# The product with w_b_out by plain and block pairs, two low parts by DMA, and a turned order of matmuls in some products

## The chip, the core and the metric

One Trainium2 chip, one of its cores. The metric is the time of one execution on the device, in microseconds. The weights are in HBM, and a kernel is given them as they are. The host lays the activations with features on rows (1024 x 576: 512 frames of a new stream and 64 of a running one, 576 columns) and turns the outputs back.

## The reference

One layer of a streaming encoder: a half-step feed-forward, a mixer with two convolution branches, a second half-step feed-forward and a norm. All of it is float32.

```python
def encoder_layer(x, ...):
    x = x + 0.5 * swiglu_ffn(rms_norm(x, ffn1_norm), ffn1_w_gate_up, ffn1_w_down)   # 1024 -> 2 * 2816 -> 1024
    h = rms_norm(x, mix_norm)
    p = h @ w_in                                                                    # 1024 -> 7 * 1024
    a_b, a_c, a_v, b_u, gate_a, gate_b = jnp.split(p, cuts, axis=-1)
    a_conv, new_a = causal_depthwise_conv(a_c * a_v, hist_a, conv_a_w)              # 3 taps
    y_a = (a_b * a_conv) @ w_a_out
    glu = b_u[..., :D_B] * jax.nn.sigmoid(b_u[..., D_B:])
    b_conv, new_b = causal_depthwise_conv(glu, hist_b, conv_b_w)                    # 31 taps
    b_act = jax.nn.silu(layer_norm(b_conv + conv_b_bias, conv_b_ln_g, conv_b_ln_b))
    y_b = b_act @ w_b_out                                                           # 1024 -> 1024
    merged = jax.nn.sigmoid(gate_a) * y_a + jax.nn.sigmoid(gate_b) * y_b
    x = x + merged @ w_out
    x = x + 0.5 * swiglu_ffn(rms_norm(x, ffn2_norm), ffn2_w_gate_up, ffn2_w_down)
    return x, new_a, new_b
```

## The kernel before

**Layout.** Features are on partitions, in 8 tiles `X[0]` to `X[7]` of 128 x 576; the 576 columns are worked in two halves of H = 288. Every matmul takes 128 x 128 of a weight as the stationary operand and one half of an activation tile as the moving one, and it writes one half of a tile of PSUM. Operands are split into a high part (rounded to the format that TensorE multiplies in one pass) and a low part (the rest), and a product is hi*hi + hi*lo + lo*hi. So one chunk (128 rows of the sum) of one output tile is six matmuls, in the order of `SIX` (line 57): weight-high by x-high and x-low of half 0, the same of half 1, then weight-low by x-high of half 0 and of half 1. That is four matmuls with one weight and two with another. `mm` (line 396) issues them, `product` (line 444) runs all chunks of one output tile (8 chunks, 48 matmuls where the sum is over 1024), and `both` (line 470) runs two output tiles chunk by chunk.

**Block products.** For the gate and up projections of the feed-forwards the kernel uses seven products in place of eight (Winograd's form of Strassen's scheme): the two by two blocks are the two output tiles (or gate and up), the two halves of the sum and the two halves of the columns. `plan_block` (line 333) makes seven units of weights for such a pair: three plain ones and four sums `s1` to `s4` that DVE adds, each with a high and a low part. `Forms` (line 602) makes the matching combinations of the activations (`combine`: four DVE operations on halves and two ScalarE copies for the high parts; `split`: two DVE subtractions for the low parts), and `block` (line 417) runs one of the seven: 4 chunks of three matmuls, all into one bank of PSUM. A pair by blocks is 7 x 12 = 84 matmuls; two tiles the plain way are 96.

**Weights.** `Stream` (line 195) holds all weights in the order of their use. SyncE loads raw tiles (six buffers); `begin` makes the high part on ScalarE and, where the unit is "dma", lets ScalarE write its negative into the low tile and GpSimd issue a DMA that adds the raw weight on top; where it is "dve", `end` subtracts on DVE. Units are made `ahead` units before their use. Prepared weights live in tiles `u` and `g` (8 each) or `act` (44, shared with activations).

**Order of the mixer.** After feed-forward 1: products `("p", 4, j)` and `("p", 3, j)`, then 1, 2, 0; then `("p", 5, j)` and `("ya", j)` in turn (the branch A product, `ya_of` writes the gated result to `M[j]`), `("p", 6, j)` (gate of branch B), `("yb", j)` with w_b_out, and `("o", j)` with w_out, which adds to `X[j]` and scales for feed-forward 2. `swish` finishes branch B on DVE and ScalarE while `("p", 6, j)` runs; its operations wait in the list `work` and are put between products by `fill` and `gb_of`. Four times, `Sum.total` (line 552) sums squares or values over partitions: four matmuls with the weight `ones_r` put between two products (in feed-forward 1 it is six shorter ones, the `room` form).

The engines run in program order; which of them waits is decided by buffers and data alone.

Of the kernel before, what the change touches and what calls it, by code (L numbers as in the profile page):

```python
# [1 line left out]

# [11 lines left out]
P = 128  # L14
# [92 lines left out]
def tile_encoder_step(  # L107
# [19 lines left out]
    tmp = ctx.enter_context(tc.tile_pool(name="tmp", bufs=6))  # L127
    rpool = ctx.enter_context(tc.tile_pool(name="rpool", bufs=1))
    mmps = ctx.enter_context(tc.tile_pool(name="mmps", bufs=4, space=bass.MemoryType.PSUM))

# [64 lines left out]
    class Stream:  # L195
# [9 lines left out]

        def raw(self, w, row0, k, col0):
            ap = w[0, row0 : row0 + k * P, col0 : col0 + P].rearrange("(k p) n -> p k n", p=P)
            self.raws.append((ap, k))
            self.last.append({})
            return len(self.raws) - 1  # L210
# [102 lines left out]
    def plan_tile(name, w, row0, ks, col0, other, home_of=None, low="dma"):  # L313
        plan[name] = []
        for k in ks:
            r = ws.raw(w, row0, k, col0)
            plan[name].append(ws.unit(r, k, home_of or home(other), low))
            row0 += k * P
# [14 lines left out]
    def plan_block(name, raws, homes, low="dma"):  # L333
# [40 lines left out]

    def plan_mixer(name, w, col):
        plan_tile(name, w, 0, (KU, KU), col, "act")

# [6 lines left out]
    for j in range(KT):  # L384
        plan_mixer(("p", 5, j), w_in, 5 * D + j * P)
        plan_mixer(("ya", j), w_a_out, j * P)
    for j in range(KT):
        plan_mixer(("p", 6, j), w_in, 6 * D + j * P)
    for j in range(KT):
        plan_mixer(("yb", j), w_b_out, j * P)  # L390
    for j in IN_TURN:
        plan_mixer(("o", j), w_out, j * P)
    plan_ffn("f2", ffn2_gu, ffn2_dn)
# [23 lines left out]
    def block(w, xs):  # L417
# [6 lines left out]
        return q  # L424


    work = []
# [16 lines left out]
    def product(name, xs, then=None, order=None, got=None, soon=None):  # L444


        if name in early:
            return early.pop(name)[:, :, :H]
        ps = psum2()
        if order or got:  # L450
            got = got or chunks(name)
            for n, k in enumerate(order or range(len(xs))):
                mm(ps, *got[k], xs[k], n == 0, n == len(xs) - 1)
        else:
            k = 0
            for n in plan[name]:
                w = ws.get(n)
                for kk in range(ws.units[n][1]):
                    mm(ps, w, kk, xs[k], k == 0, k == len(xs) - 1)
                    k += 1  # L460
                    if soon and k == 1:
                        soon()
# [39 lines left out]
    class Sum:  # L502
# [49 lines left out]
        def total(self, spans=HALVES, room=None):  # L552

            if room:
# [47 lines left out]
    class Forms:  # L602

        def __init__(self, r_g):
            self.r_g, self.b, self.t, self.parts = r_g, {}, {}, {}
# [439 lines left out]
    def b_of(j):  # L1047
# [9 lines left out]
        return then  # L1057

    for j in range(KT):
# [11 lines left out]
    def swish(i, RL, sig={}):  # L1071
# [13 lines left out]
        if 0 <= j < KT:  # L1085
            BA[j] = (BA[j], low(sig[j], BA[j]))

    def ga_of(j):
# [5 lines left out]
    def ya_of(j):  # L1094
        def then(ps):
            m = atile() if j < 4 else wtile(n=T)
            dve.tensor_tensor(halves(m), ps, halves(gates.pop(j)), op=ALU.mult)
            M.append(m)
        return then
# [35 lines left out]
    while stage[0] < 4:  # L1135
        while work:
            work.pop(0)()
        advance()
    work.extend((lambda i=i: swish(i, RL)) for i in range(KT + 2))

# [11 lines left out]
    while work:  # L1152
        work.pop(0)()
    take()

    MS = []
    for j in range(KT):
        ps = product(("yb", j), BA)
        dve.tensor_tensor(halves(SGB[j]), ps, halves(SGB[j]), op=ALU.mult)
        dve.tensor_tensor(M[j], M[j], SGB[j], op=ALU.add)  # L1160
        MS.append(split(M[j]))
# [151 lines left out]
```

## Time and profile before

| | us |
|---|---|
| median of 3 runs | 1294.79 |
| lowest and highest | 1294.35, 1294.93 |
| the profiled execution's own time | 1294.93 |
| its span, first to last instruction | 1293.2 |
| TensorE busy | 1283.2 (99%) |
| DVE, ScalarE, GpSimd busy | 893.0, 763.5, 370.2 |

The span is what the trace covers; 1.7 us of the time lie around it. A matmul's shown length is modelled and overlaps the next one's, so the pace of TensorE is read from the starts: the time from the start of one group of matmuls to the start of the next, over their number.

### The profile page before, as it was taken

What the parts mean: (1) busy time and instruction counts of PE and PEld (TensorE: products, weight loads), DVE (VectorE), ACT (ScalarE), POOL (GpSimd) and SP (SyncE); (2) the same over time, 40 slices, a digit from 0 to 9 for tenths busy, and PEclk for the clock granted to TensorE, in tenths of its full rate; (3) what the DMA queues carried; (4) which work ended last, traced back from release to release, by engine and by line L of the source; (5) the groups of instructions that cost most, each with busy time, mean ns of one, the idle gap of its engine ahead of it and who ended that gap; (6) DMA issues with size and microseconds to landing.
All of it is one profiled execution on the core that took longest, in us unless ns stands there. A gap on an engine that the chain in (4) does not pass through costs nothing.

```text
span 1293.2 us, 25663 instructions
## 1 busy us (share of the span) xinstructions
PE 1283.2 (99%) x9752; PEld 1281.8 (99%) x9752; DVE 893.0 (69%) x1477; ACT 763.5 (59%) x1353; POOL 370.2 (29%) x470
## 2 busy tenths in 40 slices
PE   9999999999999999999999999999999999999997
PEld 9999999999999999999999999999999999999997
DVE  6858668748846998898885160346857858847956
ACT  7646656645776655555454674467665655654664
POOL 0032322322333444333321322222142241241230
PEclk9999999999999999999999999999999999999999
DMA  7286786886799898787885978776697696796683
GB/s 223 66 187 150 164 183 148 178 178 152 153 196 186 172 204 167 171 170 171 175 170 121 206 158 167 168 158 140 139 176 175 149 197 148 160 209 135 160 173 93
DMA packets 285948, 213.16 MB, mean 165 GB/s; under 512 B 15360, under 2 KB 248832, under 8 KB 285824
## 3 DMA queue, kind: packets, MB, share of 16 engines
q0 software_dynamic: 57600, 95.05, 44.7%
q1 hardware_dynamic: 226480, 115.63, 31.4%
q8 instruction: 77, 1.26, 0.4%
q10 hardware_dynamic: 1744, 0.83, 0.2%
q14 instruction: 47, 0.39, 0.1%
HBM read 113.81 MB, written 2.62 MB: 90 GB/s over the span
## 4 chain that ended last, share of the span: by engine, by line
PE 88%; issue 8%; DMA 2%; POOL 1%; DVE 1%; ACT 0%; POOLq 0%; DVEq 0%; SPq 0%; ACTq 0%
PE mm L83 88%; DMA u<-raw 1%; POOL g L83 1%; POOL u L83 1%; DMA raw<-in_ffn_w_gate_up_dram 0%; DMA raw<-in_ffn_w_down_dram 0%; DMA g<-raw 0%; DVE g L83 0%; DVE tmp L83 0%; POOLq L83 0%; DVE w L83 0%; DVEq L1303 0%; ACT g L83 0%; ACT u L83 0%; DVE r L83 0%
## 5 line engine op out<-in xcount | busy, mean ns | idle before, releaser
L83 PE MATMUL mm<-act,u 128*128 128x288 f32 x4686 | 660.3, 293 | 0.2 <-DMA u<-raw 0.2
L83 PEld LDWEIGHTS mm<-act,u 128*128 128x128 f32 x4686 | 630.7, 188 | 0.4 <-DMA u<-raw 0.4
L83 PE MATMUL mm<-act,g 128*128 128x288 f32 x2778 | 399.2, 294 | 0.0
L83 PEld LDWEIGHTS mm<-act,g 128*128 128x128 f32 x2778 | 377.9, 188 | 0.0
L83 PE MATMUL mm<-act,act 128*128 128x288 f32 (+2 forms) x2244 | 306.1, 293 | 0.0
L83 PEld LDWEIGHTS mm<-act,act 128*128 128x128 f32 x2244 | 297.4, 188 | 0.3 <-ACT act L83 0.3
L83 POOL DMA_DIRECT2D u<-raw x197 | 171.7, 871 | 411.3 <-ACT u L83 300.8
L83 ACT CAST u<-raw 128x512 fp32r<-128x512 f32 (+2 forms) x203 | 116.2, 572 | 155.8 <-PE mm L83 127.3
L83 POOL DMA_DIRECT2D g<-raw x117 | 101.9, 871 | 274.4 <-ACT g L83 220.0
L83 DVE SCALAR_TENSOR_TENSOR w<-g,prm,w 128x606 f32<-128x606 f32 x232 | 179.2, 842 | 1.4 <-ACT w L83 1.4
L83 DVE TENSOR_TENSOR tmp<-mm,tmp 128x288 f32<-128x288 f32 (+1 forms) x239 | 107.4, 458 | 68.1 <-PE mm L83 53.1
L83 POOL DMA_DIRECT2D act<-raw x86 | 73.9, 859 | 195.5 <-ACT act L83 186.3
L83 ACT ACTIVATE u<-u 128x512 fp32r<-128x512 f32 (+2 forms) x197 | 116.9, 593 | 6.3
L83 DVE SCALAR_TENSOR_TENSOR tmp<-mm,r 128x576 f32<-128x576 f32 x48 | 36.3, 756 | 79.1 <-PE mm L83 79.1
L83 ACT CAST g<-raw 128x512 fp32r<-128x512 f32 (+2 forms) x126 | 68.9, 547 | 37.2 <-DMA raw<-in_ffn_w_down_dram 16.7
L83 ACT CAST u<-w 128x512 fp32r<-128x512 f32 x79 | 48.9, 619 | 63.1 <-DVE w L83 55.4
L83 ACT CAST g<-w 128x512 fp32r<-128x512 f32 x77 | 47.7, 619 | 61.6 <-DVE w L83 55.5
L83 ACT CAST act<-tmp 128x576 fp32r<-128x576 f32 x84 | 56.7, 675 | 42.7 <-DVE tmp L83 41.1
L83 DVE TENSOR_TENSOR act<-tmp,act 128x576 fp32r<-128x576 f32 x84 | 62.1, 754 | 18.2 <-ACT act L83 16.5
L83 ACT ACTIVATE g<-g 128x512 fp32r<-128x512 f32 (+2 forms) x117 | 66.4, 568 | 3.7
L83 ACT CAST act<-raw 128x512 fp32r<-128x512 f32 (+3 forms) x94 | 55.4, 592 | 12.1 <-PE mm L83 6.5
L83 DVE TENSOR_TENSOR w<-raw,raw 128x512 f32<-128x512 f32 x78 | 53.4, 684 | 10.0 <-DMA raw<-in_ffn_w_gate_up_dram 10.0
(88 smaller groups left out, 802.0 us busy)
## 6 DMA issues: line engine op xcount, KB each, us to landing
raw<-in_ffn_w_gate_up_dram SPq DMA_DIRECT2D x171, 256.0 KB, 3.4
u<-raw POOLq DMA_DIRECT2D x140, 256.0 KB, 4.0
raw<-in_w_in_dram SPq DMA_DIRECT2D x112, 256.0 KB, 3.6
act<-raw POOLq DMA_DIRECT2D x80, 256.0 KB, 4.2
raw<-in_ffn_w_down_dram SPq DMA_DIRECT2D x96, 192.0 KB, 3.6
g<-raw POOLq DMA_DIRECT2D x60, 256.0 KB, 3.8
g<-raw POOLq DMA_DIRECT2D x43, 192.0 KB, 4.4
u<-raw POOLq DMA_DIRECT2D x41, 192.0 KB, 4.4
```

Source lines behind the costliest of these rows:

```text
L83: return self.tc.keep_in_program_order(fn(*args, **kwargs))
```

## The change

Three edits.

1. **The product with w_b_out.** The eight output tiles are made in four pairs: pairs 0 and 2 plain, pairs 1 and 3 by blocks. The combinations of branch B's activations are made by `Forms` from the outputs of `swish`: pairs 0 and 1 of them in the list `work`, 2 and 3 after the gate product. The low parts of the plain pairs' weights are made on DVE. To have room, `M[j]` is now `X[j]` itself: `X[j]` is written to HBM while products 1, 2, 0 run (`kept`), and read back (`back`) when `M[j]` has been split for the product with w_out. The prepared weights of the gate product go to `u` three times of four, and the units of w_out alternate between `u` and `g` rather than `u` and `act`.
2. **Two sums' low parts.** In the first two block pairs of feed-forward 2 (i = 1, 2) the low parts of `s3` and `s4` are made by DMA rather than by DVE.
3. **Turned chunks.** `turn` orders the matmuls of two neighbouring chunks anew: the first four of the first, all six of the second, the last two of the first. `both` does it at k = 1 with its two tiles (all eight places are the down products), `product` at chunks 1 and 2 where it is the first after a `Sum.total` without `room`, and in the first product with w_out. The up product of feed-forward 2, which follows a total too, is handed its weights (`got`) and takes the other branch: it clears the mark and is not turned.

```diff
-        ], [home("g") for _ in range(7)], "dve" if (f, i) == ("f1", PLAIN[f]) else "dma")
+        ], [home("g") for _ in range(7)], "dve" if (f, i) == ("f1", PLAIN[f]) else "dma",
+            "dma" if f == "f2" and i < PLAIN[f] + 2 else "dve")
...
-                (s3, "dve", ((s3, (a11, a21)),)),
+                (s3, low_s, ((s3, (a11, a21)),)),
                 (a12, low, ()),
-                (s4, "dve", ((s4, (s2, a12)),)),
+                (s4, low_s, ((s4, (s2, a12)),)),
...
+    for i in range(KU):
+        pair = 2 * i, 2 * i + 1
+        if i % 2 == 0:
+            for j in pair:
+                plan_mixer(("yb", j), w_b_out, j * P, homes_b, "dve")
+        else:
+            plan_block(("yb", "s", i), [
+                ws.raw(w_b_out, h * P, KU, j * P, 2) for j in pair[::-1] for h in range(2)
+            ], [next(homes_b) for _ in range(7)])
     for j in IN_TURN:
-        plan_mixer(("o", j), w_out, j * P)
+        plan_tile(("o", j), w_out, 0, (KU, KU), j * P, "g")
...
+    def turn(tiles, xs):
+        (p, w, k, x), (q, v, l, z) = ((*t, x) for t, x in zip(tiles, xs))
+        for ps, u, kk, b, six in (p, w, k, x, SIX[:4]), (q, v, l, z, SIX), (p, w, k, x, SIX[4:]):
+            mm(ps, u, kk, b, False, False, six=six)
+    turned = [False]
...
         ps = psum2()
+        at, turned[0] = 1 if turned[0] else None, False
...
+                    if k == at:
+                        turn([(ps, w, kk), (ps, w, kk + 1)], xs[k : k + 2])
+                    elif at is None or k != at + 1:
+                        mm(ps, w, kk, xs[k], k == 0, k == len(xs) - 1)
...
         for k in range(len(xs)):
+            if k == 1:
+                turn([(p, *w[k]) for p, w in zip(ps, ws_)], [xs[k]] * 2)
+                continue
...
             p = psum2()
+            turned[0] = True
             span = slice(spans[0][0], spans[-1][1])
...
     for j in range(KT):
         for b, of in ((1, c_of), (2, cv_of), (0, b_of)):
             product(("p", b, j), xg, of(j))
-    M, SGB, BA = [], [], []
+        nc.sync.dma_start(kept[j], X[j])
+    M, SGB, BA = X, [], []
+    forms = Forms()
...
+    for i in range(KT + 2):
+        work.append(lambda i=i: swish(i, RL))
+        if i in (3, 5):
+            work.append(lambda p=(i - 3) // 2: forms.combine(p))
+        if i in (4, 6):
+            work.append(lambda p=(i - 4) // 2: forms.split(p))
+    ws.ahead = 4
...
+    def merged(j, c):
+        dve.tensor_tensor(M[j], M[j], c, op=ALU.add)
+        if j not in (4, 5):
+            MS[j] = high(M[j])
+            if j != KT - 2:
+                lows(KT - 2, KT - 1) if j == KT - 1 else lows(j)
...
+        for n, xs in enumerate(bs):
+            q.append(block(ws.get(plan["yb", "s", i][n]), xs))
+            if n > 0:
+                steps[n - 1]()
+        dve.tensor_tensor(half(c2, 0), q[6], u3, op=ALU.add)
+        dve.tensor_tensor(c2, c2, SGB[j + 1], op=ALU.mult)
+        merged(j + 1, c2)
...
+    plain_pair(0)
+    block_pair(1)
+    plain_pair(2)
+    back(0, 1)
+    block_pair(3)
+    back(2, 3)
...
+    turned[0] = True
     for n, j in enumerate(IN_TURN):
         ps = product(("o", j), MS)
+        if n < 2:
+            back(4 + 2 * n, 5 + 2 * n)
```

## Rows read from the trace of the kernel before

**Rows 1.** The page: busy time of the engines, and the granted TensorE clock in 40 slices of the span.

```profile
PE 1283.2 (99%) x9752; PEld 1281.8 (99%) x9752; DVE 893.0 (69%) x1477; ACT 763.5 (59%) x1353; POOL 370.2 (29%) x470
PEclk9999999999999999999999999999999999999999
```

**Rows 2.** All waits of TensorE that the trace shows (us in total, times, longest).

```profile
PE mm L83 <- POOL eps L83: 1.0, 1, 1.0
PE mm L83 <- ACT tmp L83: 0.5, 1, 0.5
PE mm L83 <- DMA u<-raw: 0.2, 1, 0.2
```

**Rows 3.** Timeline of TensorE (start, modelled length, groups of like matmuls) at the end of feed-forward 1's down products, through the first product with w_in (two rows of 24), the first total (4 matmuls), and the next product.

```profile
386.10 2.54 PE L83 MATMUL mm<-act,g 128*128 128x288 f32 x18
...
395.57 3.32 PE L83 MATMUL mm<-act,act 128*128 128x288 f32 x24
398.74 3.33 PE L83 MATMUL mm<-act,u 128*128 128x288 f32 x24
401.90 0.69 PE L83 MATMUL mm<-tmp,ones_r 128*128 128x288 f32 x4
402.43 3.28 PE L83 MATMUL mm<-act,act 128*128 128x288 f32 x24
405.55 3.28 PE L83 MATMUL mm<-act,u 128*128 128x288 f32 x24
408.67 3.28 PE L83 MATMUL mm<-act,act 128*128 128x288 f32 x24
```

**Rows 4.** The same view around the two totals of the layer norm: a row before and after the first, then a row before and after the second.

```profile
686.35 3.29 PE L83 MATMUL mm<-act,u 128*128 128x288 f32 x24
689.47 0.69 PE L83 MATMUL mm<-tmp,ones_r 128*128 128x288 f32 x4
690.00 3.32 PE L83 MATMUL mm<-act,act 128*128 128x288 f32 x24
693.16 3.32 PE L83 MATMUL mm<-act,u 128*128 128x288 f32 x24
...
715.28 0.69 PE L83 MATMUL mm<-tmp,ones_r 128*128 128x288 f32 x4
715.81 3.28 PE L83 MATMUL mm<-act,act 128*128 128x288 f32 x24
718.93 1.33 PE L83 MATMUL mm<-act,u 128*128 128x288 f32 x9
```

**Rows 5.** The same view, the product with w_b_out: its first and last of 16 rows of 24 matmuls, and the first row of the product with w_out.

```profile
796.93 3.28 PE L83 MATMUL mm<-act,act 128*128 128x288 f32 x24
...
843.73 3.28 PE L83 MATMUL mm<-act,u 128*128 128x288 f32 x24
846.85 1.33 PE L83 MATMUL mm<-act,act 128*128 128x288 f32 x9
```

**Rows 6.** The same view, the start of feed-forward 2: the total, the plain up product (two rows of 24), the first block pair (its first row of seven and the first row of the next pair), and the start of the down products.

```profile
903.02 0.69 PE L83 MATMUL mm<-tmp,ones_r 128*128 128x288 f32 x4
903.55 3.32 PE L83 MATMUL mm<-act,g 128*128 128x288 f32 x24
...
909.87 1.74 PE L83 MATMUL mm<-act,g 128*128 128x288 f32 x12
...
920.99 1.74 PE L83 MATMUL mm<-act,u 128*128 128x288 f32 x12
...
954.35 4.90 PE L83 MATMUL mm<-act,g 128*128 128x288 f32 x36
...
962.25 2.54 PE L83 MATMUL mm<-act,g 128*128 128x288 f32 x18
```

**Rows 7.** The same view, two other places where the rhythm of six is broken: the `room` total in feed-forward 1, and the last total but one at the end.

```profile
24.89 0.81 PE L83 MATMUL mm<-tmp,ones_r 128*128 128x192 f32 x6
...
27.93 3.32 PE L83 MATMUL mm<-act,u 128*128 128x288 f32 x24
31.09 3.19 PE L83 MATMUL mm<-act,g 128*128 128x288 f32 x23
...
1274.25 0.47 PE L83 MATMUL mm<-tmp,ones_r 128*128 128x304 f32 x2
1274.56 8.68 PE L83 MATMUL mm<-act,act 128*128 128x272 f32 x69
1283.08 0.62 PE L83 MATMUL mm<-acc,ones 128*128 128x272 f32 x2
```

**Rows 8.** Busy time by stretch (length, then PE, PEld, DVE, ACT, POOL with counts, granted clock, DMA share, GB/s): the gate product with w_in, the product with w_b_out, the block pairs of feed-forward 2's first group.

```profile
747.00:797.00 50.00, 50.00 (x387) 50.00 (x386) 21.80 (x33) 33.18 (x53) 12.90 (x15) 1.00 0.82 168
797.00:847.00 50.00, 50.00 (x387) 50.00 (x386) 15.91 (x21) 23.74 (x40) 13.75 (x16) 1.00 0.73 157
904.00:953.00 49.00, 49.00 (x372) 49.00 (x372) 41.94 (x75) 33.93 (x62) 13.03 (x16) 1.00 0.66 138
```

**Rows 9.** DVE's groups in the block pairs of feed-forward 2 (operation, shapes, count, busy, mean ns): steps from PSUM, low parts of combinations, low parts and sums of weights.

```profile
L83 DVE TENSOR_TENSOR tmp<-mm,tmp 128x288 f32<-128x288 f32 (+1 forms) x23 | 10.4, 463 | 4.3 <-ACT tmp L83 3.3 <-PE mm L83 1.0
L83 DVE TENSOR_TENSOR act<-tmp,act 128x576 fp32r<-128x576 f32 x8 | 5.8, 753 | 0.5
L83 DVE TENSOR_TENSOR u<-w,u 128x512 fp32r<-128x512 f32 x8 | 5.5, 684 | 0.1
L83 DVE TENSOR_TENSOR w<-raw,raw 128x512 f32<-128x512 f32 x7 | 4.8, 682 | 0.0
```

**Rows 10.** DVE's timeline at the product with w_b_out: the gating of its first tile (in brackets DVE's idle time before it, and what ended that), then the last tile's gating, its add, and the low part for w_out.

```profile
803.37 0.76 DVE L83 TENSOR_TENSOR w<-mm,w 128x576 f32<-128x576 f32 x1 [31.27 <-PE mm L83]
...
847.05 0.76 DVE L83 TENSOR_TENSOR g<-mm,g 128x576 f32<-128x576 f32 x1 [3.19 <-PE mm L83]
847.84 0.76 DVE L83 TENSOR_TENSOR w<-w,g 128x576 f32<-128x576 f32 x1
849.35 0.76 DVE L83 TENSOR_TENSOR act<-w,act 128x576 fp32r<-128x576 f32 x1 [0.74 <-ACT act L83]
```

**Rows 11.** DMA issues on SyncE's queue (KB each, us from issue to landing).

```profile
raw<-in_w_b_out_dram SPq DMA_DIRECT2D x16, 256.0 KB, 3.1
x<-in_x_dram SPq DMA_DIRECT2D x8, 288.0 KB, 5.5
```

More of the change, by code (lines that the diff above doesn't have):

```diff
@@ L1 @@
+from collections.abc import Iterator
 from contextlib import ExitStack
+from itertools import cycle
 import concourse.bass as bass
@@ L204, in __init__, with raw @@
             self.sums, self.eager = {}, False
-        def raw(self, w, row0, k, col0):
-            ap = w[0, row0 : row0 + k * P, col0 : col0 + P].rearrange("(k p) n -> p k n", p=P)
-            self.raws.append((ap, k))
+        def raw(self, w, row0, k, col0, step=1):
+            rows = w[0, row0 : row0 + k * P] if step == 1 else w[0]
+            ap = rows[:, col0 : col0 + P].rearrange("(k a p) n -> a p k n", a=step, p=P)
+            self.raws.append((ap[row0 // P if step > 1 else 0], k))
             self.last.append({})
@@ L316, in plan_tile @@
             r = ws.raw(w, row0, k, col0)
-            plan[name].append(ws.unit(r, k, home_of or home(other), low))
+            to = next(home_of) if isinstance(home_of, Iterator) else home_of or home(other)
+            plan[name].append(ws.unit(r, k, to, low))
             row0 += k * P
@@ L373, in tile_encoder_step, with plan_mixer @@
     plan_ffn("f1", ffn1_gu, ffn1_dn)
-    def plan_mixer(name, w, col):
-        plan_tile(name, w, 0, (KU, KU), col, "act")
+    def plan_mixer(name, w, col, home_of=None, low="dma"):
+        plan_tile(name, w, 0, (KU, KU), col, "act", home_of, low)
     for j in range(KT):
@@ L386, in tile_encoder_step @@
         plan_mixer(("ya", j), w_a_out, j * P)
+    few = cycle(("u", "u", "u", "act"))
     for j in range(KT):
-        plan_mixer(("p", 6, j), w_in, 6 * D + j * P)
-    for j in range(KT):
-        plan_mixer(("yb", j), w_b_out, j * P)
+        plan_mixer(("p", 6, j), w_in, 6 * D + j * P, few)
+    homes_b = iter((
+        "u", "act", "u", "act", "u", "act", "u", "act", "u", "g", "act",
+        "u", "act", "u", "g", "u", "act", "u", "g", "u", "act", "g",
+    ))
+    for i in range(KU):
[7 more added lines that the diff above has]
+            ], [next(homes_b) for _ in range(7)])
     for j in IN_TURN:
-        plan_mixer(("o", j), w_out, j * P)
+        plan_tile(("o", j), w_out, 0, (KU, KU), j * P, "g")
     plan_ffn("f2", ffn2_gu, ffn2_dn)
@@ L1057, in b_of @@
         return then
+    kept = [
+        dram.tile([P, T], F32, tag=f"kept{j}", name=f"kept{j}") for j in range(KT)
+    ]
     for j in range(KT):
@@ L1153, in tile_encoder_step, with back @@
         work.pop(0)()
+    for p in range(KU // 2, KU):
+        forms.combine(p)
     take()
[L1156 to L1161, printed above, removed]
+    for p in range(KU // 2, KU):
+        forms.split(p)
+    MS = [None] * KT
+    def back(*js):
+        for j in js:
+            nc.sync.dma_start(X[j], kept[j])
@@ new lines, in tile_encoder_step, with lows, plain_pair @@
+    ws.ahead = AHEAD_UNITS
+    bs = forms.operands(BA[::2] + BA[1::2])
+    def lows(*js):
+        for j in js:
+            MS[j] = MS[j], low(M[j], MS[j])
+    def merged(j, c):
[4 more added lines that the diff above has]
+                lows(KT - 2, KT - 1) if j == KT - 1 else lows(j)
+    def plain_pair(i):
+        for j in (2 * i, 2 * i + 1):
+            ps = product(("yb", j), BA)
+            dve.tensor_tensor(halves(SGB[j]), ps, halves(SGB[j]), op=ALU.mult)
+            merged(j, SGB[j])
@@ new lines, in block_pair, with second, first @@
+    def block_pair(i):
+        j = 2 * i
+        c1, c2, qu, uu = (ttile() for _ in range(4))
+        q1, u2, u3, u4 = half(qu, 0), half(qu, 1), half(uu, 0), half(uu, 1)
+        q = []
+        def second():
+            dve.tensor_tensor(u3, q[3], u2, op=ALU.add)
+            dve.tensor_tensor(half(c2, 1), u3, q[2], op=ALU.subtract)
+            if i == KU - 1:
+                MS[4], MS[5] = split(M[4]), split(M[5])
+        def first():
+            dve.tensor_tensor(half(c1, 1), q[5], u4, op=ALU.add)
+            dve.tensor_tensor(c1, c1, SGB[j], op=ALU.mult)
+            merged(j, c1)
+        steps = (
+            lambda: sca.copy(q1, q[0]),
+            lambda: dve.tensor_tensor(u2, q[1], q1, op=ALU.subtract),
+            lambda: dve.tensor_tensor(u4, q[2], u2, op=ALU.subtract),
+            second,
+            lambda: dve.tensor_tensor(half(c1, 0), q[4], q1, op=ALU.add),
+            first,
+        )
+        for n, xs in enumerate(bs):
[5 more added lines that the diff above has]
+        merged(j + 1, c2)
+        spare.clear()
@@ L1163, in tile_encoder_step @@
+    plain_pair(0)
[4 more added lines that the diff above has]
+    back(2, 3)
+    ss = Sum()
+    xg = [None] * KT
+    forms = Forms(R_N2)
     ss = Sum()
```

12 lines of the change are left out of this document (5 added, 7 removed).

## The prediction

> **What bounds the kernel now.** I read the page first: TensorE is busy for 99% of the span at the full granted clock, the 2.4 GHz level, and no other engine is over 69% [rows 1]. Then TensorE's waits: all that it waited for is 1.7 us, most of it at the two ends [rows 2]. So the time is the number of matmuls times their pace, and only three things move it: fewer matmuls, another pace, or a new wait.
>
> The pace has to be read from starts in the timeline, and there the reader should see what the page hides. All these matmuls have 288 columns and one granted clock, but they run at different paces. Products by `SIX` have two, which I call the short beat (130.0 ns a matmul) and the long beat (131.67). In feed-forward 1's down products and the first product with w_in, 48 matmuls take 401.90 - 395.57 = 6.33 us, 131.9 ns each, the edge of the total included; the next product takes 408.67 - 402.43 = 6.24 us, 130.0 each [rows 3]. Down products: (395.57 - 386.10)/72 = 131.5. For the long beat I use the 3.16 us per 24 matmuls from 690.00 to 693.16 [rows 4], 131.67 ns. The change of pace falls on the total: four matmuls with one weight, put between two chunks. The total at 689.47 turns short into long, the one at 715.28 turns long into short [rows 4], and the one at 903.02 turns short into long: the up product behind it takes 909.87 - 903.55 = 6.32 us [rows 6]. So TensorE has two beats, 1.67 ns a matmul apart; a run of like chunks keeps its beat for hundreds of us, and four more matmuls of one weight toggle it. Blocks have a longer one still: 920.99 - 909.87 = 11.12 us for 84, 132.4 ns [rows 6]. They are seen only where the long beat came in, and the down products behind them have it too.
>
> **Edit 1, matmuls.** The product with w_b_out takes 846.85 - 796.93 = 49.92 us for 384 matmuls, 130.0 each, all in the short beat [rows 5]. Two pairs go from 2 x 96 = 192 to 2 x 84 = 168 matmuls. 192 x 130.0 = 24.96 us become 168 x 132.4 = 22.24 us: **-2.7 us**. Bounds of the new pace: 130.0, if blocks keep the short beat (-3.1), and 132.4. I take 132.4, since that is every block in the trace. The plain pair between the two block pairs then finds the long beat: 96 x 1.67 = **+0.2 us**. Pair 0 stays at 130.0.
>
> **Edit 1, what else it moves.** All of this must stay under TensorE. DVE is busy for 15.9 of 50 us in this product [rows 8]. Added: low parts of 8 units of the plain pairs, 8 x 0.68; in the block pairs 8 sums and 8 low parts of sums, 16 x 0.68; 14 steps on halves, 14 x 0.46 [rows 9]: 22.9 us, together 38.8 in about 47.4 us, 82%. The block pairs of feed-forward 2 run with DVE at 41.9 of 49 us, 86% [rows 8], and TensorE has no wait there [rows 2], so I cost it at nothing. The combinations: 4 x (4 x 0.46 + 2 x 0.75) = 13.4 us of DVE. DVE was idle for 31.27 us before 803.37, since 772 [rows 10], and has 21.8 of 50 us in the gate product [rows 8]; the combinations are needed from about 809, so they fit. If `swish` ended only with the gate product, the last two combinations (6.7 us) would still lie under plain pair 0 (12.5 us of matmuls). `kept` and `back` are 16 more transfers of 288 KB on SyncE's queue; the like took 5.5 us to land [rows 11]. The writes wait for nothing. The reads wait for the low parts of `M[j]`, and the weight loads stand behind them; `back(4, 5)` waits longest, until late in the last block pair, but the weights then in the buffers are six units ahead, over 9 us even at a block's 1.6 us each, and `X[4]` is needed only after two products of 6.2 us. Nothing, and if a load does come late, a wait of the size of one landing (3.1 us [rows 11]). In return ten of the sixteen low parts by DMA leave GpSimd's queue.
>
> **The tightest place** is the start of the product with w_out, which needs all of `M` split. Now the low part of the last tile ends 850.11 - 846.85 = 3.3 us after the last matmul [rows 10] and is needed at the eighth chunk, 42 x 0.130 = 5.5 us after it. With the last block pair there is one half step (0.46) more on this chain, one low part (0.76) more, because tiles 6 and 7 are split together, and the gating of tile 6 ahead of it ends about 0.5 us late: 3.3 + 0.46 + 0.76 - 0.74 (the wait for ScalarE [rows 10], which the other low part now fills) + 0.45 = 4.2 us. 1.3 us are left, so nothing; if ScalarE is held by a weight copy at that moment, two operations of 0.62 us, it is even.
>
> **Edit 2.** Four low parts, 4 x 0.68 = 2.7 us, leave DVE at the start of feed-forward 2, and ScalarE and GpSimd get four more each. DVE does not hold TensorE there [rows 2, 8], so nothing either way; the room on ScalarE (33.9 of 49 us) covers 4 x 0.63.
>
> **Edit 3, the turns.** No matmul more or less; all it can move is the beat. The trace holds no turn, so its worth is bounded from both sides by the two paces: at one end all `SIX` products in the long beat go over to the short one, at the other all in the short beat to the long one. What speaks for a change to the short beat: a turn puts, behind complete chunks, four matmuls with one weight and then a complete chunk, which is just what a total does [rows 3, 4]. What speaks against: the two matmuls left over follow, and two of one weight changed the pace as well at the end: 69 matmuls of 272 columns take (1283.08 - 1274.56)/69 = 123.5 ns, near their 113.3 of columns plus the 10 that the short beat has over 120 [rows 7]. And six matmuls of 192 columns did not toggle it: the products behind have the long beat (31.09 - 27.93 = 3.16 us per 24) [rows 7]. I take it that a turn ends in the short beat. It is nearer to the totals than to the other two in shape and columns.
>
> Then, at 1.67 ns: feed-forward 1's down products, 1056 matmuls less 24 at each of the four starts, 960 x 1.67 = **-1.6**. The first product with w_in, 48: **-0.1**. The first total then finds the short beat and leaves the long one, and the turn in the next product mends it after 18 matmuls: 0. The four products from 690.00 to 715.28, 192 matmuls less 20: **-0.3**; after the second total 18 in the long beat: 0. Product with w_out: turned behind the block pair, so 130.0 as now: 0. The up product of feed-forward 2 is not turned, so 131.67 as now: 0. Feed-forward 2's down products: first three groups 768 less 72, 696 x 1.67 = **-1.2**; the last group has its own halves of 304 and 272 columns and a last total that would now toggle the other way: its 108 first matmuls give 0.1, the end may take 0.1 back: **-0.1**.
>
> **Sum.** -2.7 + 0.2 - 1.6 - 0.1 - 0.3 - 1.2 - 0.1 = -5.8 us. The profiled execution took 1294.9, 0.1 above the median of 1294.8, so I predict **1289.0** beside that median.
>
> **Rivals.**
> - *Order does not matter.* Pace would hang on columns alone, or a turn undo itself with its last two matmuls. Then the block pairs leave the long beat for the product with w_out and the first of feed-forward 2, 432 x 1.67 = +0.7, and the next total gives the up product the short beat, -0.1: -2.7 + 0.2 + 0.7 - 0.1 = -1.9, **1292.9**. For it: the 192-column total and the left-over two. Against it: three toggles at one column count and one clock. The Trainium skill, TensorE: Matmul & The Clock Gate, section "Back-to-back issue gap", puts a warm matmul alone at columns/2.4 + 2.5 ns, whatever stands before it; by that, an estimate, 288 columns are 122.5 ns and a turn is worth nothing. The trace does not agree: 130.0, 131.67 and 132.4 ns.
> - *Blocks keep the short beat.* The 17 pairs behind turned down products in each feed-forward, and the two new ones, go to 130.0: 36 x 84 x 2.4 ns = 7.3 us more, **1281.7**. For it: the last 69 matmuls, three to a chunk as in a block, have the short beat [rows 7]. Against it: it asks that blocks, which were never seen in it, hold it through changes between halves.
> - *Down products gain, the projection loses.* The turn in the down products works, so the first total now leaves the long beat; the turn inside one `product` stands at another phase (one chunk before it, not two) and fails. 402.43 to 689.47 is 2208 matmuls, +3.7; the stretch to 715 gains 0.3; then 720 matmuls +1.2, and w_out +0.7. With the rest: **about 1294.6**.
> - *The other side: a turn spoils what a total has mended.* If the down products stay at 131.67, the first total still leaves 130.0, and a turn that toggles puts the whole projection at 131.67: +3.7, after the second normal total +1.2, w_out +0.7; -2.7 + 0.2 + 3.7 + 1.2 + 0.7 = +3.1, **1297.9**. It decides as soon as a turn behind the first total ends in the long beat, for that alone is more than the block pairs save.
>
> **How the numbers follow.** Chances: forecast 0.57, order without effect 0.15, blocks at 130.0 0.08, down gains and projection loses 0.10, spoiled 0.10. 0.2%, 2.6 us, is about what a measurement can tell from no change here. Faster by more: forecast and blocks at 130.0, 0.65. Within: 0.25. Slower: 0.10. The forecast's own range is 1287.5 to 1291.0: the bounds of the new blocks' pace below, a wait of a us or two at w_out above. 1286.0 to 1294.9 takes in the forecast and the two cases above it, 0.82; the two outer ones are left out.
>
> **What would show it.** In the timeline of TensorE: rows of 12 for two stretches of about 11.1 us in the product with w_b_out, which as a whole is near 47.4 us; 3.12 us per 24 matmuls in down products, at 402 to 715 and in w_out; 2.37 us per 18 in down products would mean that the turn did nothing. In the waits: nothing new on TensorE; a wait on `act` at the first product with w_out would show that the tightest place did not hold. Wrong altogether if a row of 24 behind the first total is 3.16 us.

## The result, and the profile after

The changed kernel takes 1297.0 us (median of 18 executions, 1293.9 to 1298.3) against 1294.8 before: 1.0016 times as long, interval 1.0009 to 1.0022. The forecast was 1289.0. The profiled execution of after took 1297.2 us with a span of 1295.2, 2.0 more than before's.

No engine's load explains it. From the page of after, the answer to [rows 1]:

```profile
PE 1283.5 (99%) x9728; PEld 1281.9 (99%) x9728; DVE 922.9 (71%) x1535; ACT 768.0 (59%) x1363; POOL 365.9 (28%) x464
PEclk9999999999999999999999999999999999999999
```

TensorE has 24 matmuls fewer and the same full clock, and is busy for 0.3 us longer: the pace got worse. Where, the starts in its timeline tell. The ledger is made of differences between starts, after less before ([rows 3 to 6] and the fences below; f1 and f2 are the two feed-forwards):

| stage | forecast | measured |
|---|---|---|
| to the first total (f1 down, first w_in product) | -1.7 | 400.22 - 401.90 = -1.68 |
| first total to first total of the layer norm | 0 | 291.28 - 287.57 = +3.71 |
| between that and the second one | -0.3 | 25.83 - 25.81 = +0.02 |
| second total to the product with w_b_out | 0 | 82.71 - 81.65 = +1.06 |
| product with w_b_out | -2.5 | 47.53 - 49.92 = -2.39 |
| w_out and the first product of f2, to the total of f2 | 0 | 56.94 - 56.17 = +0.77 |
| total of f2 to its down products | 0 | 53.48 - 51.33 = +2.15 |
| f2 down products to the end | -1.3 | 2.0 less the sum above = -1.6 |

Each row compares one profiled execution with one other, so small differences are within the spread: to the first total, the ten profiled kernels with the turned pairs take 399.68 to 401.09 us, the three without them 401.90 to 402.20.

Timeline of TensorE in after, around the first total and the two of the layer norm (start, modelled length, group; against [rows 3, 4]):

```profile
397.10 3.29 PE L85 MATMUL mm<-act,u 128*128 128x288 f32 x24
400.22 0.69 PE L85 MATMUL mm<-tmp,ones_r 128*128 128x288 f32 x4
400.75 3.34 PE L85 MATMUL mm<-act,act 128*128 128x288 f32 x24
403.94 3.33 PE L85 MATMUL mm<-act,u 128*128 128x288 f32 x24
407.10 3.33 PE L85 MATMUL mm<-act,act 128*128 128x288 f32 x24
...
691.50 0.69 PE L85 MATMUL mm<-tmp,ones_r 128*128 128x288 f32 x4
692.03 3.34 PE L85 MATMUL mm<-act,act 128*128 128x288 f32 x24
...
717.33 0.69 PE L85 MATMUL mm<-tmp,ones_r 128*128 128x288 f32 x4
```

The row ahead of the first total is 3.12 us (400.22 - 397.10): the turns in the down products brought the short beat. Behind it the row with the turn is 3.19 us and the next 407.10 - 403.94 = 3.16. Behind the other two totals the ledger says the same: nothing gained between the totals of the layer norm (+0.02), and 624 matmuls x 1.67 ns = 1.04 of the 1.06 us lost behind the second. The turn inside a product did not mend what the total did. The prediction had named a row of 3.16 us behind the first total as what would make it wrong altogether.

The product with w_b_out and the start of feed-forward 2 (same view; the last number in brackets is idle time and what ended it; against [rows 5, 6]):

```profile
800.04 3.33 PE L85 MATMUL mm<-act,u 128*128 128x288 f32 x24
...
812.68 1.74 PE L85 MATMUL mm<-act,u 128*128 128x288 f32 x12
...
823.80 3.33 PE L85 MATMUL mm<-act,u 128*128 128x288 f32 x24
...
845.97 4.94 PE L85 MATMUL mm<-act,g 128*128 128x288 f32 x36
...
904.51 0.69 PE L85 MATMUL mm<-tmp,ones_r 128*128 128x288 f32 x4
...
915.00 1.82 PE L85 MATMUL mm<-act,g 128*128 128x288 f32 x12 [0.30 <-DVE tmp L85]
...
924.79 1.58 PE L85 MATMUL mm<-act,u 128*128 128x288 f32 x10 [1.36 <-DMA u<-raw]
...
957.99 4.89 PE L85 MATMUL mm<-act,g 128*128 128x288 f32 x36
```

The block pair takes 823.80 - 812.68 = 11.12 us, as forecast. (The row of 36 at 845.97 is a block's 12 and the first 24 of w_out, which so begins at 847.57.) The two waits in brackets are new: the three that before has [rows 2] lie elsewhere, at 1.0, 1246.2 and 1284.2 us.

What is late at 924.79 is a low part by DMA. The activation on ScalarE that ends the norm's root (`r<-mm`) and GpSimd's issue of that DMA, in before:

```profile
910.24 0.64 ACT L83 ACTIVATE r<-mm 128x576 f32<-128x576 f32 x1
```

```profile
917.38 0.86 POOL L83 DMA_DIRECT2D u<-raw  x1 [4.18 <-ACT tmp L83]
```

And in after, with the negatives ahead of the root:

```profile
909.68 0.63 ACT L85 ACTIVATE u<-u 128x512 fp32r<-128x512 f32 x1
...
912.02 0.63 ACT L85 ACTIVATE u<-u 128x512 fp32r<-128x512 f32 x1
912.56 0.64 ACT L85 ACTIVATE r<-mm 128x576 f32<-128x576 f32 x1
```

```profile
919.77 0.86 POOL L85 DMA_DIRECT2D u<-raw  x1 [4.25 <-ACT act L85]
```

Counted from the total, the root is at 7.22 us before and at 8.05 after, with two new negatives of 0.63 us ahead of it, those of edit 2's sums. What stands behind it is later by as much: DVE's steps (the wait of 0.30 at 915.00), and the issue, at 14.36 before and 15.26 after. The landing takes longer too. DMA issues on GpSimd's queue in that stretch of 32 us (KB each, median us from issue to landing), before and then after:

```profile
u<-raw POOLq DMA_DIRECT2D x3, 256.0 KB, 3.7
```

```profile
u<-raw POOLq DMA_DIRECT2D x3, 256.0 KB, 4.9
```

### The profile page after: what moved, and what is told of

Same layout as the page of the kernel before. It is cut to its first block, busy times and chain, and to the rows that moved or that the text cites. A ratio compares the mean times of both kernels' runs of the same rounds, so it can differ in the third digit from the quotient of the medians.

```text
span 1295.2 us, 25735 instructions
## 1 busy us (share of the span) xinstructions
PE 1283.5 (99%) x9728; PEld 1281.9 (99%) x9728; DVE 922.9 (71%) x1535; ACT 768.0 (59%) x1363; POOL 365.9 (28%) x464
## 3 DMA queue, kind: packets, MB, share of 16 engines
HBM read 116.17 MB, written 4.98 MB: 94 GB/s over the span
## 4 chain that ended last, share of the span: by engine, by line
PE 96%; DVE 1%; DMA 1%; ACT 1%; issue 0%; DVEq 0%; SPq 0%; ACTq 0%
PE mm L85 96%; DMA raw<-in_ffn_w_gate_up_dram 1%; DVE tmp L85 1%; DMA u<-raw 0%; DVE act L85 0%; ACT u L85 0%; ACT act L85 0%; DVE w L85 0%; DVE g L85 0%; ACT tmp L85 0%; ACT w L85 0%; DVE x L85 0%; ACT g L85 0%; ACT r L85 0%; DVE acc L85 0%
## 5 line engine op out<-in xcount | busy, mean ns | idle before, releaser
L85 PE MATMUL mm<-act,u 128*128 128x288 f32 x4758 | 671.2, 294 | 1.4 <-DMA u<-raw 1.4
L85 PEld LDWEIGHTS mm<-act,u 128*128 128x128 f32 x4758 | 641.5, 188 | 1.6 <-DMA u<-raw 1.6
L85 PE MATMUL mm<-act,g 128*128 128x288 f32 x3030 | 433.0, 294 | 0.3 <-DVE tmp L85 0.3
L85 PEld LDWEIGHTS mm<-act,g 128*128 128x128 f32 x3030 | 410.4, 188 | 0.5 <-issue 0.5
L85 PE MATMUL mm<-act,act 128*128 128x288 f32 (+2 forms) x1896 | 261.3, 294 | 0.3 <-DVE act L85 0.3
L85 PEld LDWEIGHTS mm<-act,act 128*128 128x128 f32 x1896 | 253.5, 188 | 0.5 <-ACT act L85 0.5
L85 POOL DMA_DIRECT2D g<-raw x126 | 110.5, 877 | 290.0 <-ACT g L85 241.6
L85 POOL DMA_DIRECT2D act<-raw x67 | 57.6, 859 | 108.1 <-ACT act L85 94.1
L85 ACT ACTIVATE g<-g 128x512 fp32r<-128x512 f32 (+2 forms) x128 | 73.4, 573 | 4.1
L85 ACT ACTIVATE tmp<-tmp 128x576 f32<-128x576 f32 x47 | 32.2, 685 | 44.4 <-DVE tmp L85 44.4
```

The source lines that it names most:

```text
L85: return self.tc.keep_in_program_order(fn(*args, **kwargs))
```

## The experiments

Theory at the outset: a turn works only from some places in the alternation of the long beat, and edit 2 makes the waits in feed-forward 2. Rival: the turn inside a product never works, because only one tile takes part in it, and the waits come from edit 1's other homes and queues.

**The place of the turn.** In `product`:

```diff
-        at, turned[0] = 1 if turned[0] else None, False
+        at, turned[0] = 2 if turned[0] else None, False
```

> The changed kernel with the turn inside a product one chunk later (chunks 2 and 3 in place of 1 and 2). Place theory: a turn gives the short beat when it starts an even number of chunks after the long beat set in, as in the down products (two chunks before it), and not when it starts an odd number after; then the stretches after the three totals and the product with w_out go to 130.0 ns: 2208 + 172 + 800 + 400 matmuls x 1.67 = 6.0 us less, about 1291.0. Tile theory: a turn works only across two output tiles and never inside one; then no change, 1297.0. Reading: 3.12 or 3.16 us per 24 matmuls behind each total.

1291.8 us, 0.9978 of before (0.9968 to 0.9988): one chunk later, the turn works. (The place of a turn is the number of chunks between the start of the long beat and the turn; it is even or odd.) Timeline of TensorE from the first row behind the first total, and at the product with w_out:

```profile
401.10 3.33 PE L85 MATMUL mm<-act,act 128*128 128x288 f32 x24
404.27 3.28 PE L85 MATMUL mm<-act,u 128*128 128x288 f32 x24
407.39 3.28 PE L85 MATMUL mm<-act,act 128*128 128x288 f32 x24
...
849.17 3.32 PE L85 MATMUL mm<-act,g 128*128 128x288 f32 x24
852.34 3.32 PE L85 MATMUL mm<-act,u 128*128 128x288 f32 x24
```

From 404.27 on rows are 3.12 us, and so behind both other totals. Only w_out stays at 3.16. The starts inside its first product show why, in ns from one matmul to the next, a line for each chunk and the sum of its six behind it where the beat is steady (780 is the short one, 790 the long one):

```
chunk 3 (turn)      131 133 127 134 132 136
chunk 4 (turn)      136 137 134 134 130 126
chunk 5 (short)     128 132 131 133 130 126    780
chunk 6 (short)     128 132 131 133 130 126    780
chunk 7             131 149 133 133 134 133
chunk 8             136 160 132 134 132 133
next    (long, b)   131 131 131 131 134 132    790
next    (long, a)   131 133 127 134 132 133    790
```

The turn works there too, and then the long beat comes back, at two gaps of some 20 and 30 ns (149 and 160 in place of 131 to 133) where the last two tiles are read. The lines also show what the places differ in: short chunks are all alike, long ones alternate between two forms, a and b, and the one behind a total that leaves the long beat is an a. A turn that begins where an a would stand (after 2 chunks, or after 2 in `both`) leaves the short beat; one that begins at a b (after 1) doesn't.

**No turn inside a product.**

```diff
-        at, turned[0] = 1 if turned[0] else None, False
+        at = None
```

> The changed kernel with turns in the down products alone; none inside a product. If the turn inside a product does nothing but shift the place in the rhythm: the projection stays at 131.67 up to the first total of the layer norm, that total then stands at an even place and gives 130.0 to the four products behind it (-0.3 us), the second takes it back; about 1296.7. If the turn inside a product is what spoils the projection: 130.0 from 402 us on, 3.7 to 4.9 us less, about 1292 to 1293.

1296.4 us, 1.0014 (1.0005 to 1.0023). The first total of the layer norm here:

```profile
691.23 0.69 PE L85 MATMUL mm<-tmp,ones_r 128*128 128x288 f32 x4
691.76 3.28 PE L85 MATMUL mm<-act,act 128*128 128x288 f32 x24
694.88 3.28 PE L85 MATMUL mm<-act,u 128*128 128x288 f32 x24
```

With no turn, 368 chunks lie between the first total and the first of the layer norm, an even number, and the total at 691.23 leaves the short beat (3.12). In after, the failed turn had moved the alternation by one chunk, and the same total left the long beat. So a turn at a wrong place costs twice: it fails, and it shifts the next total.

The starts show that totals go by the same rule. The last chunk ahead of a total and the first behind it, in before at 401.90 and in after at 691.50 (the last number ahead of a total is the step into it):

```
before, ahead  (b)       132 131 130 131 134 135
before, behind (short)   128 132 131 133 130 126    780
after,  ahead  (a)       130 134 127 134 132 131
after,  behind (a)       130 134 127 134 132 133    790
```

The 13 profiles hold 52 totals of 288 columns, and none breaks the rule: met behind a b of the long beat (14) they leave the short beat, met behind an a (9) or in the short beat (28) the long one. The one left over is met in a third beat, shown below, and leaves the long one.

**Other places, in pairs of even and odd.** Chunk 4 behind the first total, 5 and 2 behind those of the layer norm, 5 in w_out:

```diff
-        at, turned[0] = 1 if turned[0] else None, False
+        at, turned[0] = ats.pop(0) if turned[0] and not got else None, False    # ats = [4, 5, 2, 5]
```

> The changed kernel with the turn at another chunk behind each mark: 4 behind the first total, 5 behind the first total of the layer norm, 2 behind the second, 5 in the product with w_out. Theory (parity of the place decides, not the place itself): rows of 24 of 3.12 us from the fifth chunk behind the first total to the total at about 688, 3.16 us between the totals of the layer norm, 3.12 us behind the second of them, 3.16 us in the product with w_out whatever stalls there; feed-forward 2 as in the changed kernel. Time: as with all turns at chunk 2 (1291.8), plus 192 x 1.67 ns = 0.3: 1292.1. If only the distance of two chunks from the total matters: 3.16 us throughout from 402 to 690, and 1295 or more. If every turn works behind a total that leaves the long beat and only a turn right behind it fails: 3.12 us everywhere, 1291.5.

1292.1 us, 0.9980 (0.9971 to 0.9988). First behind the first total, then behind the first and the second of the layer norm:

```profile
407.93 3.28 PE L85 MATMUL mm<-act,act 128*128 128x288 f32 x24
411.05 1.20 PE L85 MATMUL mm<-act,u 128*128 128x288 f32 x8
...
698.77 3.32 PE L85 MATMUL mm<-act,u 128*128 128x288 f32 x24
701.93 3.32 PE L85 MATMUL mm<-act,act 128*128 128x288 f32 x24
...
718.27 3.28 PE L85 MATMUL mm<-act,u 128*128 128x288 f32 x24
721.39 3.28 PE L85 MATMUL mm<-act,act 128*128 128x288 f32 x24
```

Place 4 works (411.05 - 407.93 = 3.12), place 5 doesn't (3.16), place 2 does. Even and odd decide, not the distance from the total. Place 5 in w_out left 3.16 too, but a gap of 0.16 us stands in that product and could have done it alone.

**The turned pairs alone.** Before, with the turn in `both` and nothing else:

```diff
+            if k == 1:
+                turn([(p, *w[k]) for p, w in zip(ps, ws_)], [xs[k]] * 2)
+                continue
```

> The kernel before with the turn in `both` alone. Theory (a turn in a down product works, and each total then toggles the other way): f1's down products -1.6, first w_in product -0.1, 2208 matmuls behind the first total in the long beat +3.7, between the layer norm's totals -0.3, from the second one to w_out's end 1.67 ns x 1440 = +2.4, f2's down products -1.3: 1294.8 + 2.8 = 1297.6. If the totals set the beat whatever they find (the first total then leaves the short one as before): 1294.8 - 1.6 - 0.1 - 1.3 = 1291.8.

1297.4 us, 1.0021 (1.0012 to 1.0029), 0.2 from what was expected: an edit that shortens the stages it touches by some 3 us makes the kernel 2.6 us longer, since each total behind them starts from the other beat.

**Edit 2 undone, and edit 2 alone.**

```diff
-            "dma" if f == "f2" and i < PLAIN[f] + 2 else "dve")
+            "dve")
```

> The changed kernel with the low parts of all sums on DVE again (edit 2 undone). If edit 2 makes the waits at the start of feed-forward 2 (0.3 and 1.4 us, 2.1 us between the total and the down products): 1294.9 and no such wait. If the loads that `back` and the kept tiles put on SyncE's queue make them (edit 1): 1297.0 and the same waits.

1295.65 us, 1.0006 (0.9997 to 1.0015). From the total of feed-forward 2 to its down products 956.54 - 905.06 = 51.48 us, and TensorE's list of waits has none there. That is 2.0 us less than in after; the median gains 1.4, and is 0.8 above what was expected. In the profile, 0.5 us are lost ahead of the first total (400.76 against 400.22), within the spread given above.

Before, with edit 2's lines alone:

```diff
+            "dma" if f == "f2" and i < PLAIN[f] + 2 else "dve")
...
-                (s3, "dve", ((s3, (a11, a21)),)),
+                (s3, low_s, ((s3, (a11, a21)),)),
```

> The kernel before with edit 2 alone. Theory (ScalarE's negatives delay the next raw unit's copy, and its low part by DMA lands late): the pace of no product outside feed-forward 2 changes, and from the total of feed-forward 2 to its down products it takes 1 to 2 us more than before (51.3): about 1296.5, with waits of TensorE on u<-raw. As predicted on record (edit 2 costs nothing): 1294.8 and no such wait. If the wait only comes where the units of w_out were homed otherwise (edit 1), it is 1294.8 too.

1297.85 us, 1.0024 (1.0014 to 1.0034). Where TensorE waited in feed-forward 2:

```profile
913.95 1.82 PE L83 MATMUL mm<-act,g 128*128 128x288 f32 x12 [0.44 <-DVE tmp L83]
...
922.67 1.59 PE L83 MATMUL mm<-act,u 128*128 128x288 f32 x10 [0.28 <-DMA u<-raw]
...
1046.30 3.70 PE L83 MATMUL mm<-act,u 128*128 128x288 f32 x26 [1.74 <-DMA u<-raw]
```

The same two waits without edit 1: the stretch takes 955.88 - 903.32 = 52.56 us, 1.2 more than before. The rest of the 3.0 is a third wait, 1.74 us by the view and 2.0 by the starts, in the second group's down products, behind a pause in GpSimd's DMA issues. Neither after nor any other kernel has it; why edit 2 brings it there is not settled.

All profiles together: the root comes 8.0 to 8.2 us behind the total in the five kernels with edit 2, and 6.8 to 7.2 us in the eight without it. What edit 2 then costs goes with the landing of the one DMA behind it: from issue to landing it takes 4.98 us in after, 4.36 with the turn at 2, 4.01 with the other places and 3.92 with no turn inside a product, and TensorE waits for it for 1.36, 0.73, 0.39 and 0.30 us.

**Edit 1 alone.** After without edit 2 and without turns:

```diff
-            "dma" if f == "f2" and i < PLAIN[f] + 2 else "dve")
+            "dve")
...
-        at, turned[0] = 1 if turned[0] else None, False
+        at = None
...
-            if k == 1:
-                turn([(p, *w[k]) for p, w in zip(ps, ws_)], [xs[k]] * 2)
-                continue
```

> Edit 1 alone: no turn anywhere, no low parts of sums by DMA. By the prediction's sum for a turn of no effect: block pairs -2.7, plain pair +0.2, product with w_out and the first of feed-forward 2 +0.7, up product -0.1: 1292.9. If the block pairs' work on DVE or the transfers cost TensorE a wait of their own: more, by its size.

1293.8 us, 0.9995 (0.9986 to 1.0004). The first products of w_out:

```profile
847.51 3.38 PE L85 MATMUL mm<-act,u 128*128 128x288 f32 x24
850.73 3.39 PE L85 MATMUL mm<-act,g 128*128 128x288 f32 x24
```

A row is 3.22 to 3.23 us, 134.4 ns a matmul: a third beat, which begins at a gap of 0.04 us in the first product and is held for all of w_out. From the first matmul of w_out to the total of feed-forward 2 this kernel takes 57.99 us, where before takes 56.17 and after 56.94: 1.8 us of what the block pairs gave are lost. A gap of 0.02 to 0.05 us stands in the same chunk of eight of the ten kernels with edit 1, and it does not do the same in each. With no turn inside a product, one of 0.05 us led from the long beat into the short one; behind the turn at 2 the short beat became the long one; in after the long one stayed. What a gap leads into is open. The block pairs' own pace is 820.59 - 809.47 = 11.12 us again, here entered from the short beat.

Edit 1 is not free in feed-forward 2 either. With it alone, TensorE waits there for another low part by DMA:

```profile
930.79 1.60 PE L85 MATMUL mm<-act,u 128*128 128x288 f32 x10 [0.52 <-DMA u<-raw]
```

The six kernels with edit 1 and without edit 2 take 51.5 to 52.2 us from the total to the down products; the two with neither (before, and the turned pairs alone) take 51.3 and 51.2. So the rival was right in part, with up to 0.9 us; what in edit 1 makes that low part late, no run shows.

**Both mends.** After with both edits:

```diff
-            "dma" if f == "f2" and i < PLAIN[f] + 2 else "dve")
+            "dve")
...
-        at, turned[0] = 1 if turned[0] else None, False
+        at, turned[0] = 2 if turned[0] else None, False
```

> The changed kernel with two edits: the turn behind a total starts at chunk 2, and the low parts of s3 and s4 in feed-forward 2 are made on DVE again. Theory (a turn leaves the long beat only from an even place, and edit 2 alone makes the waits in feed-forward 2): 1291.8, as measured with the turn at chunk 2, less the 1.9 us by which feed-forward 2 from its total to its down products got shorter when edit 2 was undone (53.4 to 51.5): 1289.9. If the two mends are not independent (another beat into feed-forward 2 makes another wait there): 1291 to 1292. If edit 2 costs nothing: 1291.8.

1290.4 us (1289.6 to 1295.2), 0.9973 (0.9962 to 0.9983); a second time 1290.3 (1290.0 to 1290.5), 0.9965 (0.9952 to 0.9977). The two mends add. The profiled execution of the first was the one of 1295.2 us, and shows what can follow from a single wait. ScalarE ahead of the root, then TensorE:

```profile
402.31 0.62 ACT L85 CAST u<-raw 128x512 fp32r<-128x512 f32 x1 [2.01 <-DMA raw<-in_w_in_dram]
```

```profile
434.63 1.85 PE L85 MATMUL mm<-act,u 128*128 128x288 f32 x13
436.82 1.73 PE L85 MATMUL mm<-act,u 128*128 128x288 f32 x11 [0.34 <-DVE act L85]
438.38 3.32 PE L85 MATMUL mm<-act,act 128*128 128x288 f32 x24
441.55 3.32 PE L85 MATMUL mm<-act,u 128*128 128x288 f32 x24
```

A raw tile of w_in landed late, ScalarE stood for 2.0 us, DVE got the root 4.4 us behind the total (1.4 in before), and one low part came late: 0.6 us. From there to the first total of the layer norm all rows are 3.16 us. That total, met from the long beat, left the short one, and the turn behind it, which now started from the short beat, left the long one. The second total and its turn did the same.

> The kernel with both mends once more, beside the two that follow from it. In its first profile one late load of w_in held a low part back at 436 us, a gap of 0.6 us, and all products from there to the first total of the layer norm ran in the long beat, in an execution of 1295.2 us where the others had 1289.6 to 1292.2. Theory (the gap set the beat): an execution without a gap there has rows of 3.12 us from 402 to 688 and takes 1290; one with it 1294 to 1295. If the beat behind a total differs from execution to execution by itself, rows of 3.16 us appear without a gap ahead of them.

In the second profile there is no such gap, and rows are 3.12 us from 404 to the total at 687.93. That the gap set the beat rests on these two executions; no run made such a gap on its own.

**w_out.** Two ways to keep the short beat there, both on top of the two mends. One more turn, behind the gap:

```diff
+        if name == ("o", IN_TURN[1]):
+            at = 1
```

> The kernel with both mends and one more turn, at chunk 1 of the second product with w_out. Theory (the gap of 0.15 us in the first product with w_out puts TensorE back into the long beat, and a turn from an even place behind it takes it out again): rows of 24 of 3.12 us from the second product with w_out to the total of feed-forward 2, 366 x 1.67 ns = 0.6 us less than with both mends (1290.4): 1289.8. If what keeps w_out in the long beat is something of that product (its weights' tiles, its DMA traffic) and not the gap: 3.16 us per row and 1290.4.

1289.7 us (1289.6 to 1289.8), 0.9961 (0.9948 to 0.9973), the shortest of all and below both kernels. So it is not w_out's own weights or traffic that hold the long beat there:

```profile
848.28 3.32 PE L85 MATMUL mm<-act,g 128*128 128x288 f32 x24
851.44 3.28 PE L85 MATMUL mm<-act,u 128*128 128x288 f32 x24
854.56 3.28 PE L85 MATMUL mm<-act,g 128*128 128x288 f32 x24
```

The first two products as one turned pair, so that the late low parts are needed twice as late:

```diff
+        if n == 0:
+            pair = both([("o", i) for i in IN_TURN[:2]], MS)
+        ps = pair[n] if n < 2 else product(("o", j), MS)
```

> The kernel with both mends, and the first two products with w_out run as one turned pair, chunk by chunk, so that the last tiles' low parts are needed twice as late (the fourteenth of sixteen chunks, about 10 us behind the last block pair, not 5). Theory (a low part that comes a few tenths late makes the gap, and the gap the long beat): no gap, rows of 3.12 us in all of w_out, 0.1 us of gap and 0.7 us of beat less than with both mends: 1289.6. If the gap has another cause than the low part: it stays, and 1290.4.

1290.7 us, 0.9968 (0.9956 to 0.9979): a miss. The pair needs the weights of the second tile twice as early, and their low part is late instead, 1.48 us. So no run took the gap away, and that it brings the long beat is read from the starts alone:

```profile
845.49 5.26 PE L85 MATMUL mm<-act,g 128*128 128x288 f32 x38 [1.48 <-DMA g<-raw]
```

## Why the prediction was wrong

**What bounds the kernel: right.** Pace, not load, decided. Of the ledger's six differences of more than a microsecond, four are carried by the two beats and the 1.67 ns between them; the other two are the matmuls saved (-2.39) and the waits in feed-forward 2 (+2.15).

**Edit 1's matmuls: right.** -2.39 us against -2.5. Pair 0 came in the long beat too, 96 x 1.67 ns = 0.16 us that the sum did not have. "Blocks keep the short beat" falls: a block pair takes 11.12 us whichever beat is ahead of it.

**"A turn ends in the short beat": the step that failed.** The prediction asked only which beat a turn ends in, and judged by its likeness to a total. The runs show that turn and total alike end in the short beat from an even place of the long beat's alternation, in the long one from an odd place and from the short beat. In the down products that gave -1.68 to the first total, as forecast. Behind the totals the turn stood after one chunk, an odd place. That is the third rival, by its own remark on the phase and with its price for the long stretch (+3.7); it had a chance of 0.10. Its 1294.6, with the 2.15 us of feed-forward 2 and without the 0.3 us that it let the stretch between the layer norm's totals gain, makes 1297.05; 1297.0 was measured. What spoke for it could be read in the trace of before: its totals and its changes of beat were taken from rows of 24, and the starts inside a chunk, where a and b can be seen, I never read.

"Order does not matter" (1292.9) falls as well: same matmuls, clock and columns, and 1296.4, 1297.0 or 1291.8 us by whether and where a turn stands inside a product. The 122.5 ns set beside that rival are for a matmul alone; here every matmul has a weight load of its own (9728 of each), so no run tests that figure.

**Edit 2 "at nothing": wrong, 2 us.** The working compared busy shares: DVE does not hold TensorE, ScalarE has room. But the moved work lands ahead of one activation on ScalarE on which DVE and the next DMA wait in turn. Two operations of 0.63 us, in a stretch where ScalarE is idle for 15 of 49 us [rows 8], made that activation 0.8 us later, and with the four more DMAs landings took 4.9 us in place of 3.7. The profiles show both at once; no run parts the order on ScalarE from the longer landings.

**The tightest place: the size was off.** The low parts were to be done 4.2 us after the last block's matmuls; DVE's timeline shows the end at 853.12, 5.5 us after 847.57, just when they are needed:

```profile
845.91 1.43 DVE L85 TENSOR_TENSOR act<-x,act 128x576 fp32r<-128x576 f32 x2 [1.61 <-ACT act L85]
847.26 0.82 DVE L85 TENSOR_TENSOR tmp<-mm,tmp 128x288 f32<-128x288 f32 x2
...
851.54 1.58 DVE L85 TENSOR_TENSOR act<-x,act 128x576 fp32r<-128x576 f32 x2
```

The split of tiles 4 and 5, put into the last block pair, waits for ScalarE and holds DVE until 847.3; that term was missing, and the working's 0.5 us for the gating of tile 6 was 2 us. The wait itself is next to nothing: one matmul, at 853.41, starts 148 ns after the one ahead of it in place of 131. (The 0.3 us on `act` that stand new in after's list of waits are at 4.9 us, far from here.) Nor does it make the +0.77 of this stage: the turn in w_out stood at an odd place, after one chunk, and the long beat was there before the gap. Where the turn stood at an even place, the price of the gap is the beat behind it, 1.67 ns a matmul.

**Feed-forward 2's down products: near, in part by luck.** -1.6 against -1.3, but some 0.5 us of it is a wait of before that after does not have; the starts around it are 0.46 us longer than in a steady row:

```profile
1246.18 3.70 PE L83 MATMUL mm<-act,u 128*128 128x288 f32 x26 [0.19 <-DMA u<-raw]
```

The kernel with edit 1 alone, which has no turn, gains the same 0.5 us there. So the turns gave about 1.2 us against the 1.3 worked out.

## What to carry to other kernels

Where one engine is busy all the time, read its pace from starts inside one repeat of the loop, not from group means; a difference of 1% that holds for hundreds of microseconds is a state, and a change of order or a wait of a fraction of a microsecond can switch it. Before moving work to an engine with idle time, look for the one operation on it that others wait for, and count what will stand ahead of that; busy shares don't show it. Try a reordering at two neighbouring places before judging it.

## What the runs showed of the hardware

At one granted clock (1.00 of the 2.4 GHz level) and 288 columns, chunks of six run at 130.0, 131.67 or 134.4 ns a matmul, and blocks of three to a chunk at 132.4. The beats of chunks of six last until something breaks the rhythm: four matmuls of one weight, a turn, or a gap (some of 0.02 to 0.05 us at w_out, one of 0.6 us in the projection). In the long beat chunks alternate between two forms, and from the 130.0 beat every one of 28 totals of 288 columns led into it. What inside TensorE alternates, what a gap leads into, and what sets the third beat, no run here shows.
